# FOX projections of four heads as Strassen chunks in a hybrid decoder block

## The chip, the cores and the metric

The kernel runs on one core of a Trainium2 chip. Its time is the device time of one execution in microseconds (us). The kernel before took 986.61 us, median of 3 runs (986.29 to 989.09).

## The reference

One decoder block on a batch of 512 tokens with 1024 channels, all in float32. The branch A is a gated delta rule (GDN), branch B is an attention with forgetting (FOX); both have 8 heads of 128 channels. One projection makes the inputs of both.

```python
u = rmsnorm(x, norm_mix_g)
proj = u @ w_in
(gq, gk, gv, gz, ga, gb, fq, fk, fv, ff, gate_a, gate_b) = jnp.split(proj, split_idx, axis=-1)
qkv = silu(causal_depthwise_conv(concat([gq, gk, gv]), gdn_conv_w))
o_a = gated_delta_rule_chunked(qh, kh, vh, g, beta)        # qh, kh: l2norm of the heads of qkv
o_a = rmsnorm(o_a, gdn_norm_g) * silu(gz)
y_a = o_a @ w_proj_gdn
o_b = forgetting_attention(rmsnorm(fq), rmsnorm(fk), fv, log_sigmoid(ff + f_bias))
y_b = o_b @ w_proj_fox
h = x + (sigmoid(gate_a) * y_a + sigmoid(gate_b) * y_b) @ w_out
out = h + square(relu(rmsnorm(h) @ w_up)) @ w_down
```

`fq`, `fk` and `fv` of heads 0 to 3 are 12 of the blocks of 128 columns of `w_in`; they are what the change computes in another way.

## The kernel before

**Precision and weight units.** A float32 operand is split into a high part (rounded by a cast on ACT) and a low part (the rest, a subtraction on DVE), and a product is the sum of three: hi by hi, hi by lo, lo by hi. Weights come in units of 128 x 1024. `seq` (L151) lists all units in the order of their use. `unit` fetches the next one, splits up to two units ahead of it (`LA_SPLIT`) and loads up to three ahead (`LA_RAW`). The split halves live in four buffers each (pool `whl`), the raw units in three (`wraw`). L256 is the cast, L257 the subtraction.

**Dense projections.** `dense` (L269) multiplies one unit with all 512 tokens: 24 matmuls of 512 columns (L275, L276 with the high weights, L279 with the low ones), into one of three PSUM banks that take turns. `project` uses it for one of q, k, v of a GDN head and then runs the convolution: ACT L596, three DVE steps L599 that read the bank, silu on ACT. `zgate` uses it for one head's z gate. While u isn't complete, z gates are made from the unscaled x (`xh`, `xl`) and multiplied with the norm on DVE afterwards (L1080); the first `NZX` are made so.

**u.** `normalise` (L411) scales x on POOL, makes the high parts of u on ACT (L289), the low ones on DVE (L290, tiles `ulo`), and stores x scaled to DRAM (`ud`). `factors_u` (L427) loads it back as `ux`, scales it on ACT (L436), adds and subtracts quarters on DVE (L448) and splits the sums (L286, L287). These are the sums of u that Strassen's products need.

**Strassen chunks.** A chunk is a projection to 512 columns for all 512 tokens. As a 2 x 2 problem of blocks it takes seven products P1 to P7 in place of eight. `stream` (L981) runs them: a product is one weight unit and 24 matmuls of 256 columns (L1011) into a kept PSUM bank; after it a quarter of the result is copied out (ACT, L991) or added to what is there (DVE, L993). Four weight blocks of a chunk are stored so that each factor is the last one plus another block: P1 and P2 are plain loads on SP's queue, and P5, P6, P4 (on P1) and P3, P7 (on a plain load) are made by DMAs of POOL's queue that add to the raw unit in SBUF (L219) once it has been split.

**FOX projections before.** Heads 0 to 3 go through `fox_pair` (L950), two heads at a time: three panels of 256 columns, each of two weight units and four blocks of 128 tokens, 24 matmuls of 256 columns per block (L961, L962, L964). Heads 4 to 7 are three chunks of `stream`, followed by four chunks of the gates.

**The order.** The program runs tasks (Python generators) that are advanced by `tick` beside the main line: `head` (transposes, decay products kk and kq), `group_chain` (the inversion of the triangular matrices by 31 column steps of two DVE instructions, L681 and L683, and then the scan), `fox_worker` (attention of FOX heads). The main line is: z gates 0 to 5; GDN group 0 (heads 0 to 3); FOX pair 0; start of `factors_u`; FOX pair 1; z gates 6 and 7; GDN group 1; the stream of seven chunks with the first merges; merges; MLP. Which instruction stands where on each engine is decided when the program is built, by the framework's planner with its own timeline; on the chip each engine then runs its list in that order. `INV_STEP` tells after how much estimated DVE work the inversion of each group pauses until the next `tick`.

Of the kernel before, what the change touches and what calls it, by code (L numbers as in the profile page):

```python
# [15 lines left out]
P = 128  # L16
# [14 lines left out]
NZX = 6  # L31
DC = 2
IN_AT = 6
# [3 lines left out]
NZ1 = 6  # L37
# [3 lines left out]
INV_STEP = (2500, 900)  # L41


def hybrid_block(tc, a, out):
# [99 lines left out]
    def store_late(dst, src):  # L144

        for _ in range(LATE):
# [5 lines left out]
    seq += [("w_gdn", i) for i in range(12)] + [("w_fox", i) for i in range(12)]  # L152
    seq += [("w_z", i) for i in range(NZ1, H)] + [("w_gdn", 12 + i) for i in range(12)]
# [3 lines left out]
    NST = 7  # L157
    STREAM = [("P1", 0), ("P2", 0), ("P5", 0), ("P1", 1), ("P3", 0), ("P6", 0), ("P2", 1), ("P7", 0), ("P5", 1),
              ("P4", 0), ("P3", 1), ("P6", 1)]
    STREAM += [e for c in range(2, NST)  # L160
               for e in (("P1", c), ("P2", c), ("P7", c - 1), ("P5", c), ("P4", c - 1), ("P3", c), ("P6", c))]
    STREAM += [(None, 0), ("P7", NST - 1), (None, 1), ("P4", NST - 1)]
    seq += [(p, ("w_st", c, 0)) if p else ("w_pg", c) for p, c in STREAM]
# [786 lines left out]
    def fox_pair(hp):  # L950
        vts = ([], [])
        for pn in range(3):
            us = [unit("w_fox"), unit("w_fox")]
            pg2 = [page(s="fqk"), page(s="fqk")]
            for t2 in range(2):
                ps = mmps("fx")
                for tb in (2 * t2, 2 * t2 + 1):
                    o = ps[:, (tb % 2) * 256:(tb % 2 + 1) * 256]
                    for k in range(KT):
                        w = us[k // 4][0][:, (k % 4) * 256:(k % 4 + 1) * 256]  # L960
                        mm(o, uhi[k][:, cs(tb)], w, start=(k == 0), stop=False)  # L961
                        mm(o, ulo[k][:, cs(tb)], w, start=False, stop=False)  # L962
                    for k in range(KT):
                        mm(o, uhi[k][:, cs(tb)], us[k // 4][1][:, (k % 4) * 256:(k % 4 + 1) * 256], start=False,  # L964
                           stop=(k == KT - 1))
                    if tb % 2 == 0:
                        tick()
                if pn < 2:
                    act.copy(pg2[t2], ps)
                else:  # L970
                    for j in range(2):
                        (vec.tensor_copy if j else act.copy)(
                            v3(pg2[j][:, 2 * t2 * P:(2 * t2 + 2) * P], 2), v3(ps[:, :], 2)[:, :, cs(j)])
                tick()
            if pn < 2:
                fq.append((2 * hp + pn, pg2, vts[pn]))
            else:
                for v, x in zip(vts, pg2):
                    v += [x[:, cs(c)] for c in range(NCH)]

    def stream(parts, other):  # L981
# [13 lines left out]
        for p, c in STREAM:  # L995
# [143 lines left out]
    v45, v67 = ([], []), ([], [])  # L1139
# [380 lines left out]
```

## Time and profile before

| | |
|---|---|
| median of 3 runs | 986.61 us |
| profiled execution, its own time | 985.26 us |
| its span, first to last instruction | 983.6 us |
| granted TensorE clock | 1.00 |
| PE busy | 971.4 us, 6545 matmuls |
| DVE busy | 714.8 us |
| ACT busy | 602.4 us |
| POOL busy | 243.5 us |

By stage, from the trace: the norm and six z gates end at 48.28 us, GDN group 0 at 126.75, the FOX pairs at about 218, z gates 6 and 7 and group 1 at 328, the stream at about 548, and the rest runs to 983.6. In these six stretches PE was busy for 45.74 of 48.28, 77.84 of 78.47, 91.63 of 92.25 (to 219), 105.13 of 109.00, 219.57 of 220.00 and 431.44 of 435.60 us.

In rows of the profile, PE is TensorE's matmul, DVE VectorE, ACT ScalarE, POOL GpSimd, SP SyncE. A group's row gives line, engine, operation, output and inputs, shape and count, then the busy time and mean ns of one, then the idle time before it and who ended it. Durations of neighbouring matmuls overlap, since they are pipelined, so what one costs is read from the distance of starts. `[1.74 <-DVE conv L599]` is idle time of the engine just before the instruction and what it waited for.

### The profile page before, as it was taken

What the parts mean: (1) busy time and instruction counts of PE and PEld (TensorE: products, weight loads), DVE (VectorE), ACT (ScalarE), POOL (GpSimd) and SP (SyncE); (2) the same over time, 40 slices, a digit from 0 to 9 for tenths busy, and PEclk for the clock granted to TensorE, in tenths of its full rate; (3) what the DMA queues carried; (4) which work ended last, traced back from release to release, by engine and by line L of the source; (5) the groups of instructions that cost most, each with busy time, mean ns of one, the idle gap of its engine ahead of it and who ended that gap; (6) DMA issues with size and microseconds to landing.
All of it is one profiled execution on the core that took longest, in us unless ns stands there. A gap on an engine that the chain in (4) does not pass through costs nothing.

```text
span 983.6 us, 17196 instructions
## 1 busy us (share of the span) xinstructions
PE 971.4 (99%) x6545; PEld 875.7 (89%) x6545; DVE 714.8 (73%) x1205; ACT 602.4 (61%) x1048; POOL 243.5 (25%) x236
## 2 busy tenths in 40 slices
PE   9999999999999999999999999999999999999998
PEld 7878899998877999999999888889989989988986
DVE  6877768557577789854656625889897697698596
ACT  7766454676455687777666522578855765666761
POOL 1555020020623613512230004412021121121110
PEclk9999999999999999999999999999999999999999
DMA  7647653456338776756887835688798888888884
GB/s 265 219 142 216 180 157 108 129 193 204 118 104 240 175 162 160 190 131 156 241 194 204 288 107 164 121 187 166 199 174 202 189 173 208 179 174 203 187 166 119
DMA packets 93442, 174.38 MB, mean 177 GB/s; under 512 B 8016, under 2 KB 49200, under 8 KB 93360
## 3 DMA queue, kind: packets, MB, share of 16 engines
q1 hardware_dynamic: 78928, 120.85, 38.3%
q0 software_dynamic: 14432, 52.44, 30.5%
q8 instruction: 51, 0.84, 0.3%
q14 instruction: 31, 0.25, 0.1%
HBM read 152.25 MB, written 21.02 MB: 176 GB/s over the span
## 4 chain that ended last, share of the span: by engine, by line
PE 91%; DVE 4%; ACT 2%; DMA 2%; issue 1%; SPq 0%; DVEq 0%
PE mlp L1171 35%; PE st L1011 13%; PE mm L279 8%; PE mm L275 7%; PE mm L276 7%; PE fx L964 2%; PE fx L961 2%; PE fx L962 2%; PE fo L944 2%; PE sc L919 1%; PE pT L935 1%; DVE lo L257 1%; DMA ux<-ud 1%; DVE ulo L290 1%; PE v L797 1%; PE o L818 1%
## 5 line engine op out<-in xcount | busy, mean ns | idle before, releaser
L1402 ACT CAST hi<-draw 128x1024 fp32r<-128x1024 f32 x124 | 130.1, 1050 | 118.4 <-PE mlp L1171 102.5
L1409 DVE TENSOR_TENSOR lo<-draw,hi 128x1024 fp32r<-128x1024 f32 x124 | 151.4, 1222 | 44.7 <-ACT hi L1402 41.8
L256 ACT CAST hi<-raw 128x1024 fp32r<-128x1024 f32 (+1 forms) x62 | 62.7, 1020 | 91.3 <-PE mm L276 67.5
L1171 PE MATMUL mlp<-hi,shi 128*128 128x512 f32 x280 | 109.6, 391 | 0.1
L1171 PE MATMUL mlp<-hi,slo 128*128 128x512 f32 x280 | 109.2, 390 | 0.0
L1171 PE MATMUL mlp<-lo,shi 128*128 128x512 f32 x280 | 109.1, 389 | 0.0
L257 DVE TENSOR_TENSOR lo<-raw,hi 128x1024 fp32r<-128x1024 f32 (+1 forms) x62 | 75.8, 1228 | 28.6 <-PE mm L279 12.5
L1171 PE MATMUL mlp<-shi,lo 128*128 128x256 f32 x448 | 90.4, 283 | 0.0
L1171 PE MATMUL mlp<-shi,hi 128*128 128x256 f32 x448 | 90.4, 283 | 0.0
L1171 PE MATMUL mlp<-slo,hi 128*128 128x256 f32 x448 | 90.4, 283 | 0.0
L275 PE MATMUL mm<-uhi,hi 128*128 128x512 f32 x208 | 82.3, 396 | 3.9 <-DVE conv L599 3.9
L276 PE MATMUL mm<-ulo,hi 128*128 128x512 f32 x208 | 81.6, 392 | 0.0
L257 DVE TENSOR_TENSOR lo<-sraw,hi 128x1024 fp32r<-128x1024 f32 x49 | 60.7, 1239 | 21.9 <-ACT hi L256 19.0
L1171 PEld LDWEIGHTS mlp<-shi,hi 128*128 128x128 f32 x448 | 70.7, 192 | 0.9
L256 ACT CAST hi<-sraw 128x1024 fp32r<-128x1024 f32 x49 | 51.4, 1048 | 30.4 <-PE st L1011 17.3
L1171 PEld LDWEIGHTS mlp<-shi,lo 128*128 128x128 f32 x448 | 69.9, 192 | 0.0
L1171 PEld LDWEIGHTS mlp<-slo,hi 128*128 128x128 f32 x448 | 69.9, 192 | 0.0
L1171 PEld LDWEIGHTS mlp<-hi,shi 128*128 128x128 f32 x280 | 52.6, 188 | 11.2 <-issue 0.7
L1171 PEld LDWEIGHTS mlp<-lo,shi 128*128 128x128 f32 x280 | 52.6, 188 | 11.0
L1171 PEld LDWEIGHTS mlp<-hi,slo 128*128 128x128 f32 x280 | 52.6, 188 | 10.4
L599 DVE SCALAR_TENSOR_TENSOR conv<-mm,c_conv,conv 128x509 f32<-128x509 f32 (+2 forms) x72 | 52.3, 743 | 10.4 <-ACT conv L596 9.5
L219 POOL DMA_DIRECT2D draw<-w_d x30 | 26.3, 876 | 129.7 <-DVE lo L1409 127.4
(335 smaller groups left out, 2452.9 us busy)
## 6 DMA issues: line engine op xcount, KB each, us to landing
draw<-w_u POOLq DMA_DIRECT2D x32, 512.0 KB, 5.7
draw<-w_d POOLq DMA_DIRECT2D x32, 512.0 KB, 5.7
sraw<-w_st POOLq DMA_DIRECT2D x28, 512.0 KB, 6.0
draw<-w_d SPq DMA_DIRECT2D x26, 512.0 KB, 4.5
raw<-w_gdn SPq DMA_DIRECT2D x24, 512.0 KB, 3.7
draw<-w_u SPq DMA_DIRECT2D x24, 512.0 KB, 4.3
sraw<-w_st SPq DMA_DIRECT2D x21, 512.0 KB, 5.0
hd<-hd SPq DMA_DIRECT2D x34, 256.0 KB, 5.6
```

The lines of the kernel that those rows point to most:

```text
L219: nc.gpsimd.dma_start(raw, a[w][c, q, s_], accum_op=ALU.add)
L256: act.copy(hi[:, c], raw[:, c])
L257: vec.tensor_tensor(lo[:, c], raw[:, c], hi[:, c].bitcast(F32), op=ALU.subtract)
L275: mm(o, w, rhi(k), start=(k == 0), stop=False)
L276: mm(o, w, rlo(k), start=False, stop=False)
L279: mm(o, lo[:, k * cols:(k + 1) * cols], rhi(k), start=False, stop=(k == KT - 1))
L599: vec.scalar_tensor_tensor(y[:, s:], ps[:, :T - s], cw[:, i:i + 1], y[:, s:], op0=ALU.mult, op1=ALU.add)
L944: mm(po[:, cs(i)], vt[c], st[i][:, cs(c)], start=(c == 0), stop=(c == i))
L1011: mm(o, u, w, start=first and t == 0 and k == 0 and j == 0 and x is hi, stop=x is lo and k == 3, skip_group_check=True)
L1171: return (lambda *args, **kw: tc.keep_in_program_order(f(*args, **kw))) if self.pinned[0] else f
L1402: pact.copy(hi, raws[m][0])
L1409: pvec.tensor_tensor(lo, raws[m][0], hi[:, :].bitcast(F32), op=ALU.subtract)
```

## The change

Three chunks, with the weights of heads 0 to 3, go in front of the list of chunks, and `stream` takes its order of products as an argument. It now runs twice: chunks 0 to 2 between the two GDN groups, where the FOX pairs were, with z gates 6 and 7 in the two places that the second stream gives to merges; and chunks 3 to 9 where the stream was. `fox_pair` and `w_fox` are gone. `factors_u` starts after head 1 of group 0 and has to be finished before the first stream. The z gate of head 5 moves behind group 0, where u is complete. `IN_AT` is 9 in place of 6 because chunks are numbered from the new ones. The inversion of group 0 pauses after as little work as that of group 1.

```diff
-NZX = 6
+NZX = 5
-IN_AT = 6
+IN_AT = 9
-NZ1 = 6
+NZ1 = 5
-INV_STEP = (2500, 900)
+INV_STEP = (900, 900)
...
-    seq += [("w_gdn", i) for i in range(12)] + [("w_fox", i) for i in range(12)]
-    seq += [("w_z", i) for i in range(NZ1, H)] + [("w_gdn", 12 + i) for i in range(12)]
+    seq += [("w_gdn", i) for i in range(12)] + [("w_z", i) for i in range(NZ1, H - 2)]
...
+    STREAMS = chunks(0, 3), chunks(3, 10)
+    seq += [(p, ("w_st", c, 0)) if p else ("w_z", H - 2 + c) for p, c in STREAMS[0]]
+    seq += [("w_gdn", 12 + i) for i in range(12)]
+    seq += [(p, ("w_st", c, 0)) if p else ("w_pg", c) for p, c in STREAMS[1]]
...
-    def gdn_group(g, box):
+    def gdn_group(g, box, also=None):
...
+            if also and i == also[0]:
+                also[1]()
...
-    def fox_pair(hp):
...
-        for p, c in STREAM:
+        for p, c in order:
...
-    ch0 = gdn_group(0, box)
-    fox_pair(0)
-    fu = start(factors_u())
-    fox_pair(1)
+    fus = []
+    ch0 = gdn_group(0, box, (1, lambda: fus.append(start(factors_u()))))
+    fu, = fus
+    zs = list(range(NZ1, H))
+    while len(zs) > 2:
+        zgate(zs.pop(0))
+    finish(fu)
+    v45, v67, v01, v23 = [([], []) for _ in range(4)]
+    parts = [fox_chunk((None, v01), (0, v01[0])), fox_chunk((2, v23[0]), (1, v01[1])), fox_chunk((3, v23[1]), (None, v23)),
+             fox_chunk((None, v45), (4, v45[0])), fox_chunk((6, v67[0]), (5, v45[1])), fox_chunk((7, v67[1]), (None, v67))]
+    stream(STREAMS[0], parts, lambda: zgate(zs.pop(0)))
     start(decays(1, box, ch0))
     hold[0] = True
-    for h in range(NZ1, H):
-        zgate(h)
     ch1 = gdn_group(1, box)
     hold[0] = False
-    finish(fu)
...
-    stream(parts, merge_gdn)
+    stream(STREAMS[1], parts, merge_gdn)
```

What the planner makes of it, at three places. First PE at the start of GDN group 0, behind the z gate of head 4. `xs`, `hi` and `lo` in the inputs are x, `uhi` and `ulo` are u. Before, the z gate of head 5 stands here:

```order
L275 MATMUL mm_594<-xs_197,hi_518 128x512
L276 MATMUL mm_594<-xs_197,hi_518 128x512
L275 MATMUL mm_594<-xs_198,hi_518 128x512
L276 MATMUL mm_594<-xs_198,hi_518 128x512
L275 MATMUL mm_594<-hi_228,hi_518 128x512
L276 MATMUL mm_594<-lo_229,hi_518 128x512
```

Now it is the first projection of head 0, with the second one mixed in:

```order
L279 MATMUL mm_596<-uhi_182,hi_518 128x512
L280 MATMUL mm_596<-ulo_190,hi_518 128x512
L279 MATMUL mm_596<-uhi_183,hi_518 128x512
L279 MATMUL mm_647<-uhi_179,hi_553 128x512
L280 MATMUL mm_647<-ulo_187,hi_553 128x512
L280 MATMUL mm_596<-ulo_191,hi_518 128x512
L279 MATMUL mm_596<-uhi_184,hi_518 128x512
L279 MATMUL mm_647<-uhi_180,hi_553 128x512
L280 MATMUL mm_596<-ulo_192,hi_518 128x512
```

The first user of u moved 24 matmuls forward on PE; `ulo_187` to `ulo_194` are the eight tiles of u's low half.

Second, PE behind group 0. Before, a FOX block:

```order
L279 MATMUL mm_1267<-uhi_186,lo_1136 128x512
L961 MATMUL fx_1323<-hi_1206,uhi_179 128x256
L962 MATMUL fx_1323<-hi_1206,ulo_187 128x256
L961 MATMUL fx_1323<-hi_1206,uhi_180 128x256
L962 MATMUL fx_1323<-hi_1206,ulo_188 128x256
```

Now P1 of chunk 0, behind the z gate of head 5 (`mm_1349`):

```order
L283 MATMUL mm_1349<-uhi_186,lo_1218 128x512
L986 MATMUL st_1423<-hi_1284,uhi_179 128x256
L986 MATMUL st_1423<-hi_1284,uhi_180 128x256
L986 MATMUL st_1423<-hi_1284,uhi_181 128x256
L986 MATMUL st_1423<-hi_1284,uhi_182 128x256
L986 MATMUL st_1423<-hi_1284,ulo_187 128x256
```

A weight unit now serves 24 matmuls in place of 48, and the next product needs the next unit. Third, DVE at the same time in the program. Before, with FOX units (`lo`), convolutions and the decay products of head 3:

```order
L599 SCALAR_TENSOR_TENSOR conv_1244<-mm_1212,c_conv,conv_1244 128x509
L650 SCALAR_TENSOR_TENSOR am_1289<-kq_1284,ssk_1163,em_826 128x128 x4
L257 TENSOR_TENSOR lo_1316<-raw_1313,hi_1315 128x1024
L599 SCALAR_TENSOR_TENSOR conv_1303<-mm_1267,c_conv,conv_1303 128x511
L599 SCALAR_TENSOR_TENSOR conv_1303<-mm_1267,c_conv,conv_1303 128x510
L599 SCALAR_TENSOR_TENSOR conv_1303<-mm_1267,c_conv,conv_1303 128x509
```

Now, with the units of the products (`sraw`) and the sums of u (`ux`):

```order
L261 TENSOR_TENSOR lo_1418<-sraw_1221,hi_1417 128x1024
L603 SCALAR_TENSOR_TENSOR conv_1261<-mm_1223,c_conv,conv_1261 128x509
L291 TENSOR_TENSOR lo_1270<-ux_1244,hi_1269 128x512
L452 TENSOR_TENSOR ux_1245<-ux_1161 128x256
L452 TENSOR_TENSOR ux_1245<-ux_1163 128x256
L291 TENSOR_TENSOR lo_1310<-ux_1245,hi_1309 128x512
L654 SCALAR_TENSOR_TENSOR am_1318<-kq_1313,ssk_1174,em_791 128x128 x4
L261 TENSOR_TENSOR lo_1458<-sraw_1421,hi_1457 128x1024
L452 TENSOR_TENSOR ux_1245<-ux_1244,ux_1161 128x256
L603 SCALAR_TENSOR_TENSOR conv_1332<-mm_1290,c_conv,conv_1332 128x511
```

The convolutions of the last head now stand behind splits and sums that were elsewhere before or not there at all.

More of the change, by code (lines that the diff above doesn't have):

```diff
@@ L151, in hybrid_block, with chunks @@
     seq = [("w_ab", 0)] + [("w_z", i) for i in range(NZ1)]
-    seq += [("w_gdn", i) for i in range(12)] + [("w_fox", i) for i in range(12)]
-    seq += [("w_z", i) for i in range(NZ1, H)] + [("w_gdn", 12 + i) for i in range(12)]
[L157 to L163, printed above, removed]
+    seq += [("w_gdn", i) for i in range(12)] + [("w_z", i) for i in range(NZ1, H - 2)]
+    def chunks(c0, c1):
+        o = [("P1", c0), ("P2", c0), ("P5", c0), ("P1", c0 + 1), ("P3", c0), ("P6", c0), ("P2", c0 + 1), ("P7", c0),
+             ("P5", c0 + 1), ("P4", c0), ("P3", c0 + 1), ("P6", c0 + 1)]
+        o += [e for c in range(c0 + 2, c1)
+              for e in (("P1", c), ("P2", c), ("P7", c - 1), ("P5", c), ("P4", c - 1), ("P3", c), ("P6", c))]
+        return o + [(None, 0), ("P7", c1 - 1), (None, 1), ("P4", c1 - 1)]
+    STREAMS = chunks(0, 3), chunks(3, 10)
+    seq += [(p, ("w_st", c, 0)) if p else ("w_z", H - 2 + c) for p, c in STREAMS[0]]
+    seq += [("w_gdn", 12 + i) for i in range(12)]
+    seq += [(p, ("w_st", c, 0)) if p else ("w_pg", c) for p, c in STREAMS[1]]
     seq += [("w_pg", i) for i in range(2, KT)] + [("w_pf", i) for i in range(KT)]
@@ L948, in fox_worker, with stream @@
             stores.append(start(store_late(obd[h], o)))
-    def fox_pair(hp):
[L951 to L981, printed above, removed]
+    def stream(order, parts, other):
         bank = {}
@@ L1137, in merge_gdn @@
         tick()
-    v45, v67 = ([], []), ([], [])
-    parts = [fox_chunk((None, v45), (4, v45[0])), fox_chunk((6, v67[0]), (5, v45[1])), fox_chunk((7, v67[1]), (None, v67))]
     parts += [gate_chunk(i, to) for to in (sga, mg) for i in range(2)]
-    stream(parts, merge_gdn)
+    stream(STREAMS[1], parts, merge_gdn)
     ot2 = start(outputs_in2())
```

13 lines of the change are left out of this document (4 added, 9 removed).

## The prediction

> **What bounds the kernel now.** I read the head of the page first, then the engines of the chain that ended last, then the waits of PE in front of matmuls (us in total, times, longest).
>
> ```profile
> span 983.6 us, 17196 instructions
> PE 971.4 (99%) x6545; PEld 875.7 (89%) x6545; DVE 714.8 (73%) x1205; ACT 602.4 (61%) x1048; POOL 243.5 (25%) x236
> PE 91%; DVE 4%; ACT 2%; DMA 2%; issue 1%; SPq 0%; DVEq 0%
> PE mm L275 <- DVE conv L599: 3.9, 2, 2.1
> PE cum L511 <- DVE gf L506: 0.6, 1, 0.6
> ```
>
> PE is busy for 971.4 of 983.6 us and carries 91% of the chain. So a change can do two things: take matmuls away, or make or end a wait of PE, and all waits in the span are only 12.2 us. DVE at 714.8 us is second; it matters where a stage makes it work without pause. The profiled execution took 985.26 us (1.66 around the span); the median, 986.61, lies 1.35 above. My sum goes against 985.26, and 1.35 is added at the end.
>
> **Term 1, the matmuls.** The PE timeline (start, us, instruction) at the first FOX block and at the first Strassen product, and the groups of the FOX lines:
>
> ```profile
> 126.75 0.28 PE L961 MATMUL fx<-hi,uhi 128*128 128x256 f32 x1
> 128.67 1.12 PE L964 MATMUL fx<-lo,uhi 128*128 128x256 f32 x8
> 129.63 0.60 PE L119 MATMUL ktm<-ident,conv 128*128 128x128 f32 x4
> ...
> 327.99 0.64 PE L1011 MATMUL st<-hi,uhi 128*128 128x256 f32 x4
> 330.86 0.38 PE L119 MATMUL ktm<-ident,conv 128*128 128x128 f32 x2
> ...
> L961 PE MATMUL fx<-hi,uhi 128*128 128x256 f32 x192 | 48.5, 289 | 0.0
> L962 PE MATMUL fx<-hi,ulo 128*128 128x256 f32 x192 | 47.8, 284 | 0.0
> L964 PE MATMUL fx<-lo,uhi 128*128 128x256 f32 x192 | 28.4, 286 | 0.0
> ```
>
> A FOX block of 24 matmuls runs from 126.75 to 129.63: 2.88 us, 0.120 each. A product, also 24 of the same size, runs from 327.99 to 330.86: 2.87, 0.1196 each. Printed durations (0.28) overlap; starts give the price. Removed: 3 x 192 = 576. Added: 3 chunks x 7 products x 24 = 504. Difference 72 x 0.12 = **-8.6 us**. These matmuls were back to back on PE, so nothing hid them.
>
> **Term 2, the start of group 0.** The z gate of head 5 moves behind group 0. Its 24 matmuls cost the same there (and it loses the DVE multiplication L1080, 0.68). But it was also the work between the norm and the first user of its output. PE there, and DVE making the low halves of u:
>
> ```profile
> 42.73 0.40 PE L275 MATMUL mm<-xs,hi 128*128 128x512 f32 x1
> 48.28 0.39 PE L275 MATMUL mm<-uhi,hi 128*128 128x512 f32 x1
> 53.15 0.43 PE L511 MATMUL cum<-gf,upper 128*128 128x64 f32 x2 [0.63 <-DVE gf L506]
> ...
> 44.19 0.74 DVE L290 SCALAR_TENSOR_TENSOR ulo<-x,c_norm_mix_g,uhi 128x512 fp32r<-128x512 f32 x1
> 46.09 1.41 DVE L290 SCALAR_TENSOR_TENSOR ulo<-x,c_norm_mix_g,uhi 128x512 fp32r<-128x512 f32 x2
> 47.55 0.74 DVE L290 SCALAR_TENSOR_TENSOR ulo<-x,c_norm_mix_g,uhi 128x512 fp32r<-128x512 f32 x1
> 48.61 0.74 DVE L290 SCALAR_TENSOR_TENSOR ulo<-x,c_norm_mix_g,uhi 128x512 fp32r<-128x512 f32 x1
> 49.27 0.68 DVE L1080 TENSOR_TENSOR proj<-mm,rb 128x512 f32<-128x512 f32 x1
> ```
>
> Group 0 began at 48.28; now it can begin at 42.73. The L290 rows from 44.19 make tiles 3, 4 and 5, 6, 7 of the low half (order on DVE and ACT unchanged to here), done at 44.93, 46.83, 47.50, 48.29 and 49.35. PE takes one of its 512-wide matmuls per 0.23 us (24 from 42.73 to 48.28). In the order, tile 3 comes after 7 matmuls: 42.73 + 1.6 = 44.3, so it waits 0.6. Tile 4 comes after 4 more: 44.93 + 0.92 = 45.85, waits 1.0. Tiles 5 to 7 then come within 0.2 of being ready, because a second projection is mixed in. Some 0.1 for each hand-over: **+2.0 us**; ends 0 (all early) and 6.6 (nothing overlapped: 49.35 - 42.73).
> **Term 3.** The 0.63 us that PE waited at 53.15 for gf goes, since PE now arrives two later at the same place of its order: **-0.6** (0 to -0.6).
>
> **Term 4, DVE in the first stream.** The FOX pairs asked little of DVE: 60.86 of 92.25 us (third of the pairs after the span, by PE, PEld, DVE, ACT, POOL).
>
> ```profile
> 126.75:219.00 92.25, 91.63 (x930) 89.55 (x929) 60.86 (x147) 52.97 (x107) 14.27 (x13) 1.00 0.48 149
> 345.00:400.00 55.00, 55.00 (x438) 52.52 (x437) 51.21 (x137) 43.60 (x93) 16.57 (x17) 1.00 0.70 161
> L257 DVE TENSOR_TENSOR lo<-sraw,hi 128x1024 fp32r<-128x1024 f32 x49 | 60.7, 1239 | 21.9 <-ACT hi L256 19.0
> L287 DVE TENSOR_TENSOR lo<-ux,hi 128x512 fp32r<-128x512 f32 x8 | 6.3, 791 | 4.9 <-ACT hi L286 4.9
> L448 DVE TENSOR_TENSOR ux<-ux,ux 128x256 f32<-128x256 f32 x12 | 5.3, 480 | 0.1
> L599 DVE SCALAR_TENSOR_TENSOR conv<-mm,c_conv,conv 128x509 f32<-128x509 f32 x24 | 17.8, 743 | 0.5
> L993 DVE TENSOR_TENSOR fqk<-fqk,st 128x512 f32<-128x512 f32 x9 | 6.1, 672 | 2.5 <-ACT fqk L991 2.5
> L681 DVE TENSOR_TENSOR tmp<-E,X 128x126 f32<-128x126 f32 x6 | 1.7, 286 | 0.1
> 113.35 1.23 DVE L257 TENSOR_TENSOR lo<-raw,hi 128x1024 fp32r<-128x1024 f32 x1 [2.08 <-PE mm L279]
> 114.49 0.16 DVE L617 TENSOR_SCALAR ssk<-ssk 128x4 f32<-128x4 f32 x1
> ```
>
> In place of 12 weight units there are 21, each split by an ACT cast and a DVE subtraction: 9 x 1.24 = 11.2 us more on DVE. The sums of u (16 L448 at about 0.48 and 8 L287 at 0.79: 14) move ahead, into group 0 and the stream's start. Their eight loads from DRAM pass SP's queue in group 0, where three raw buffers stand ahead of use; they are needed some 30 us later. Nine evictions by addition (0.67) take the place of four copies, 5 us more at most. All this comes to 30 us in a stage with 31 us of pause. ACT, with 52.97 of 92.25, gets nine casts; POOL, with 14.27, twelve DMA issues: both have room.
> I counted the DVE order between two rows: from behind the split of the z unit ahead of the stream, to the split of the 19th product. There are 131 instructions: 19 splits (23.5 us), 12 sums (5.8), 7 splits of them (5.5), 12 conv steps (8.9), 7 evictions (4.7), 41 column steps of the inversion at about 0.29 (11.9), and the heads' and attention's own (18.7): 79 us by group means. A row starts about 0.08 before the printed end of the last (48.61 + 0.74 against 49.27 above), so 131 rows take about 69 by starts. PE's work between the uses of the same two splits is 58 us (19 products of 2.87, the rest transposes and attention). DVE's lead is about 14 us: a unit split from 113.35 is first used by its low half at 128.67, and the 2.08 us ahead of that split was a wait for a free buffer. So 69 to 79 stand against 58 + 14 = 72: from 3 us spare to 7 short. The tightest place is the second product, whose bank is freed by group 0's last conv step, 42nd of these rows: by my sum DVE is there between 0.5 ahead and 4 late. A DVE without pause need not stall PE: in 345 to 400 it was busy for 51.21 of 55.00, PE for all 55.00. I take **+1.5**; ends 0 and 12.4 (the last rival).
>
> **Term 5, conv waits of group 1.**
>
> ```profile
> 286.43 0.47 PE L275 MATMUL mm<-uhi,hi 128*128 128x512 f32 x1 [1.74 <-DVE conv L599]
> 308.32 0.47 PE L275 MATMUL mm<-uhi,hi 128*128 128x512 f32 x1 [2.13 <-DVE conv L599]
> ```
>
> Both waits of L275, 1.74 and 2.13, are PE waiting for a bank that a conv step on DVE still reads; DVE had paused before each (for the sums of ACT and for buffers) and then had a head's whole work at once. In the new order the decay matrices of group 1 and its heads' products stand later and closer together, so both bursts remain in some form; by hand I find about 0.8 and 2: **-0.9**, ends -3.9 (both gone) and +4 (doubled).
> **Term 6, the second stream.** The wider spread of group 0's column steps and attention pushed behind put 94.9 us of DVE (group means) beside 92.5 of PE in its first part, before 86.9 beside 87.3. The buffers allow three products of lead, 8.6 us, so it should hide: **+0.5**, ends 0 and 3. The tail (gates, merge, MLP) has the same order at the same distances: 0; without its cover it would wait as long as group 1's chain comes late, and 29 us of products lie between.
> Sum: -8.6 + 2.0 - 0.6 + 1.5 - 0.9 + 0.5 = -6.1, 979.2 for the profiled execution, **980.5 us** against the median.
>
> **One rule against the change.** Two rows at the same time:
>
> ```profile
> 277.48 2.33 DVE L257 TENSOR_TENSOR lo<-raw,hi 128x1024 fp32r<-128x1024 f32 x1 [1.10 <-PE mm L279]
> 277.43 1.30 POOL L588 TENSOR_TENSOR eb<-em,row 128x512 f32<-128x512 f32 x1
> ```
>
> The split took 2.33 instead of 1.24 while POOL multiplied: 1.1 us lost. The Trainium skill, "SBUF — State Buffer", section "Who interferes with whom", says that a DVE instruction with two SBUF inputs and a GpSimd instruction that reads SBUF exclude each other for a whole instruction; this pair of rows agrees. By that rule all the added splits and sums are open to such collisions; rival (c) has the price.
>
> **Rivals.** (a) **No difference**: the first stream stalls 6 us, at the second product and again at the sixth, whose weight comes out of two accumulations one after the other.
>
> ```profile
> L219 POOL DMA_DIRECT2D sraw<-w_st x28 | 24.8, 886 | 92.1 <-DVE lo L257 64.6 <-DVE X L683 12.7 <-DVE fsm L931 9.0
> sraw<-w_st POOLq DMA_DIRECT2D x28, 512.0 KB, 6.0
> ```
>
> Each such step may start only when DVE has split the weight below it, and then takes 0.89 to issue and 6.0 to land; POOL waited 64.6 us for such splits already (L219's idle time). A late DVE is passed on to PE about 7 us later. For it: the -3 to +7 above. Then -6.1 + 4.5 = -1.6, and about 985. Against it: in 345 to 400 the same chain ran beside a full DVE.
> (b) **Better**: the stream hides all and both conv waits vanish: -8.6 + 2.0 - 0.6 - 3.9 = -11.1, 975.5. For it: DVE's pauses of 2.08 before 113.35 are room.
> (c) **Slower**: DVE becomes the bound of the first stream. If the means (79) hold, because POOL blocks the splits as at 277.48, and the lead is only the three products that the buffers give (8.6), PE waits 79 - 58 - 8.6 = 12.4: -8.6 + 1.4 + 12.4 - 0.4 = +4.8, 991.4. It decides from about 8 us of waiting in the stretch. The order has nine POOL tensor operations beside these rows; nine collisions at 1.1 make 10, just the distance between 69 and 79. Against it: the mean of the 49 product splits, 1.239, is next to the single undisturbed 1.23 at 113.35, so few of them met POOL.
> (d) The change not doing what it says: the order has 72 matmuls fewer, so 0.01.
>
> **How the numbers follow.** Forecast 0.56 (977.5 to 983.6: the small terms by their nearer ends), (a) 0.20, (b) 0.14, (c) 0.09, rest 0.01. The range 975 to 988 leaves out (c), the lower part of (b) and the top of (a). Within 0.3% (983.65 to 989.57), about what a measurement of this kernel can tell from no change: (a), 0.20. Faster: forecast and (b), 0.70. Slower: (c) and the rest, 0.10.
>
> **What would show it.** Term 1: 72 fewer matmuls, 504 more rows on the product line, at 0.12 each. Term 2: first projection of group 0 near 42.7 with waits on ulo of 1 to 3 us. Term 4: in the 60 us after the last projection of group 0, waits of products on conv or lo under 3 us in total, with DVE over 85% busy; (a) shows 6, (c) over 10 and many L257 rows above 1.5 us. Term 5: conv waits in group 1 of 1 to 4 us. I am wrong if PE's total idle time grows by more than 6 us, or if it grows in a place that I called hidden.

## The result: slower by 0.8%, and the profile after

The changed kernel takes 992.85 us (median of 6 runs, 992.03 to 996.08), the kernel before 986.3 us (6 runs, 984.68 to 989.09). The ratio is 1.0076, with a 95% interval of 1.0061 to 1.0091. The forecast was 980.5 us; the difference to it is 12.3 us. The profiled execution of the changed kernel has a span of 990.6 us, 7.0 more than before. Two lines of its page (busy time, share of the span and instructions of each engine):

```profile
span 990.6 us, 17122 instructions
PE 968.1 (98%) x6473; PEld 869.3 (88%) x6473; DVE 725.7 (73%) x1218; ACT 614.3 (62%) x1059; POOL 254.2 (26%) x248
```

And the three longest of PE's waits in it (engine, tile and line that wait, what ended the wait; us in total, times, longest):

```profile
PE st L986 <- DVE fqk L968: 3.6, 1, 3.6
PE st L986 <- ACT fqk L966: 2.9, 3, 1.6
PE mm L279 <- DVE conv L603: 2.5, 1, 2.5
```

There are 72 matmuls fewer, as forecast, but PE's busy time fell by 3.3 us, not by 8.6, and the waits are others: most are not in the first stream but inside group 1 and at the start of the second stream. The stages show it. These are the windows (stretch, its length, then PE, PEld, DVE, ACT and POOL busy, the granted clock, the DMA share and GB/s) of the kernel before and then of the changed one:

```profile
125.00:200.00 75.00, 74.38 (x780) 72.17 (x780) 51.37 (x130) 41.00 (x84) 13.37 (x12) 1.00 0.42 124
280.00:360.00 80.00, 76.13 (x491) 68.45 (x490) 63.99 (x131) 50.19 (x122) 31.59 (x27) 1.00 0.69 177
```

```profile
125.00:200.00 75.00, 73.23 (x632) 70.53 (x630) 67.14 (x149) 49.43 (x93) 22.35 (x22) 1.00 0.80 179
280.00:360.00 80.00, 69.60 (x426) 61.57 (x425) 53.61 (x104) 47.59 (x112) 41.71 (x35) 0.94 0.63 152
```

In 125 to 200, where the first stream runs, DVE went from 51.37 to 67.14 of 75 us and PE lost 1.15 us. In 280 to 360, from the middle of group 1 into the second stream, PE lost 6.5 us more than before, and the clock was 0.94. For a sum over the span I took each step from one matmul's start to the next one's, minus the median step, over all runs of this document, of matmuls of the same shape into the same tile. What is above the median is called lost time here, by wait or by slow matmuls (us):

| stretch | 0 to 125 | 125 to 200 | 200 to 280 | 280 to 360 | from 360 | sum |
|---|---|---|---|---|---|---|
| before | 5.2 | 0.3 | 0.3 | 4.6 | 3.0 | 13.4 |
| changed | 6.5 | 1.9 | 1.3 | 15.7 | 3.4 | 28.9 |

So 15.5 us of new loss stand against 8.6 us of matmuls saved, which makes the 7 us by which the span grew, and 11.1 of them lie in 280 to 360. In the PE timeline of the changed kernel there (start, busy time of the group in us, line, operation, tiles, shape, count, and in brackets the wait ahead of it and what ended it):

```profile
298.19 0.77 PE L279 MATMUL mm<-uhi,hi 128*128 128x512 f32 x1 [2.47 <-DVE conv L603]
299.61 0.63 PE L280 MATMUL mm<-ulo,hi 128*128 128x512 f32 x1
...
324.54 0.71 PE L986 MATMUL st<-hi,uhi 128*128 128x256 f32 x4 [1.27 <-DVE conv L603]
332.75 0.33 PE L905 MATMUL fkT<-ident,fqk 128*128 128x128 f32 x1 [1.25 <-DVE AT L645]
337.31 1.23 PE L986 MATMUL st<-hi,uhi 128*128 128x256 f32 x4 [3.58 <-DVE fqk L968]
342.42 0.64 PE L986 MATMUL st<-hi,hi 128*128 128x256 f32 x4
```

The second stream starts at 324.54; before it was 327.99, so up to there the change is still 3.45 us ahead. Then PE waits 1.25 and 3.58 us, and behind the second wait the matmuls run at little more than half speed: 24 of them from 337.31 to 342.42, 0.213 us each where 0.120 is usual, 2.2 us more. The granted clock is 0.50 from 335.35 to 342.17 and 1.00 from 342.20 to 346. The same at 298.19: seven matmuls take about 0.43 each in place of 0.23.

Why DVE was late at 337 is read from the order of the heads. The products kk of heads 4, 5 and 6 of group 1 stand on PE at these times before and after:

```profile
281.37 1.05 PE L639 MATMUL kk<-conv 128*128 128x128 f32 x8
298.77 1.05 PE L639 MATMUL kk<-conv 128*128 128x128 f32 x8
320.70 1.05 PE L639 MATMUL kk<-conv 128*128 128x128 f32 x8
```

```profile
308.12 1.06 PE L643 MATMUL kk<-conv 128*128 128x128 f32 x8
311.74 1.06 PE L643 MATMUL kk<-conv 128*128 128x128 f32 x8
317.67 1.05 PE L643 MATMUL kk<-conv 128*128 128x128 f32 x8
```

Three heads that were 17 and 22 us apart now stand 4 and 6 us apart. Each needs rows from DRAM through three buffers, two products on POOL and eight on DVE. Two pieces of the chain of waits of the changed kernel through this stretch:

```profile
315.06 9.86 DMA row<-rowd
325.07 1.31 POOL conv L656
```

Its POOL timeline there, and its DVE timeline:

```profile
325.06 1.30 POOL L656 TENSOR_TENSOR conv<-conv,row 128x512 f32<-128x512 f32 x1 [2.48 <-DMA row<-rowd]
326.31 3.03 POOL L895 TENSOR_TENSOR fqk<-fqk,fss 128x512 f32<-128x512 f32 x2
330.08 1.45 POOL L592 TENSOR_TENSOR eb<-em,row 128x512 f32<-128x512 f32 x1
```

```profile
331.57 1.12 DVE L645 SCALAR_TENSOR_TENSOR AT<-kk,ssk,eb 128x128 f32<-128x128 f32 x4 [3.13 <-POOL eb L592]
336.58 0.67 DVE L968 TENSOR_TENSOR fqk<-fqk,st 128x512 f32<-128x512 f32 x1
```

A row load took 9.86 us, and POOL stood 2.48 us for it with its other work queued behind: the product that reads the row, two products `fqk` in 3.03 us and the issue of a weight step. So POOL reached the next head's `eb` only at 330.08; DVE waited 3.13 us for that at 331.57, with decay products, a split, convolution steps and the eviction `fqk` queued behind, and PE waited for that eviction until 337.31. That these loads and POOL's queue are what the closeness of the heads costs is read from this trace; no run changes the loads or their buffers alone.

### The profile page after: what moved, and what is told of

It reads as the page before. It is cut to its first block, busy times and chain, and to the rows that moved or that the text cites. A ratio compares the mean times of both kernels' runs of the same rounds, so it can differ in the third digit from the quotient of the medians.

```text
span 990.6 us, 17122 instructions
## 1 busy us (share of the span) xinstructions
PE 968.1 (98%) x6473; PEld 869.3 (88%) x6473; DVE 725.7 (73%) x1218; ACT 614.3 (62%) x1059; POOL 254.2 (26%) x248
## 4 chain that ended last, share of the span: by engine, by line
PE 91%; DMA 3%; DVE 2%; ACT 1%; issue 1%; POOL 1%; SPq 0%; POOLq 0%; ACTq 0%; DVEq 0%
PE mlp L1148 36%; PE st L986 19%; PE mm L279 8%; PE mm L280 8%; PE mm L283 8%; PE fo L950 2%; DMA row<-rowd 2%; PE sc L925 2%; PE pT L941 1%; DMA sraw<-w_st 1%; PE o L822 1%; PE v L801 1%; PE S L810 1%; DMA raw<-w_z 1%; DVE ulo L294 1%
## 5 line engine op out<-in xcount | busy, mean ns | idle before, releaser
L261 DVE TENSOR_TENSOR lo<-sraw,hi 128x1024 fp32r<-128x1024 f32 x70 | 87.4, 1249 | 24.1 <-ACT hi L260 17.4
L260 ACT CAST hi<-sraw 128x1024 fp32r<-128x1024 f32 x70 | 73.2, 1047 | 48.0 <-PE st L986 26.0
L279 PE MATMUL mm<-uhi,hi 128*128 128x512 f32 x216 | 86.4, 402 | 2.6 <-DVE conv L603 2.5
L280 PE MATMUL mm<-ulo,hi 128*128 128x512 f32 x216 | 85.9, 398 | 1.1 <-DVE ulo L294 1.1
L260 ACT CAST hi<-raw 128x1024 fp32r<-128x1024 f32 (+1 forms) x50 | 50.5, 1013 | 56.3 <-PE mm L280 45.3
L261 DVE TENSOR_TENSOR lo<-raw,hi 128x1024 fp32r<-128x1024 f32 (+1 forms) x50 | 59.1, 1182 | 29.2 <-ACT hi L260 13.9
L223 POOL DMA_DIRECT2D sraw<-w_st x40 | 35.5, 888 | 141.5 <-DVE lo L261 53.4
L1148 PEld LDWEIGHTS mlp<-lo,shi 128*128 128x128 f32 x280 | 52.6, 188 | 11.1
```

Source lines behind the costliest of these rows:

```text
L223: nc.gpsimd.dma_start(raw, a[w][c, q, s_], accum_op=ALU.add)
L260: act.copy(hi[:, c], raw[:, c])
L261: vec.tensor_tensor(lo[:, c], raw[:, c], hi[:, c].bitcast(F32), op=ALU.subtract)
L279: mm(o, w, rhi(k), start=(k == 0), stop=False)
L280: mm(o, w, rlo(k), start=False, stop=False)
L1148: return (lambda *args, **kw: tc.keep_in_program_order(f(*args, **kw))) if self.pinned[0] else f
```

## The experiments

All ratios are against runs of the kernel before on the same chip. Two theories were left at the start. **A**: the change of `INV_STEP` makes group 0's inversion and scan late; group 1's decay matrices wait for the end of that chain. **B**: the added splits and sums are too much for DVE.

### The pauses of the inversion

```diff
 # the changed kernel, pauses of 2500 (and, in another kernel, of 1500)
-INV_STEP = (900, 900)
+INV_STEP = (2500, 900)
```

> The changed kernel with one number put back: the inversion of group 0 pauses after 2500 instead of 900 units of DVE work. Theory A (the many pauses make group 0's inversion and scan end late, so the decay matrices of group 1 come late, the decay products of heads 4 to 6 stand close together, and their DVE work holds up the second stream): in the order the first decay matmul of group 1 moves forward by 25 us of PE work and the kk products of heads 4 to 6 are 14 and 20 us apart instead of 4 and 6; the 11 us that the changed kernel loses between 320 and 360 us go, and the time is 978 to 983 us. Rival B (DVE is over its limit because of the added splits and sums): the column steps now press into the first stream in longer pieces, PE waits more there, and the time stays at 990 us or above.

Measured: 992.59 us, ratio 1.0068 (1.0045 to 1.0090). The heads are spread and the loss in 280 to 360 is 2.4 us, as A said; but the time is that of the changed kernel, as B said. The loss has moved into 125 to 200, 16.7 us, and most of it is one wait, for the inversion's transposed result, with some 2 us of slow matmuls behind it. In its waits of PE:

```profile
PE Qp L711 <- DVE Xd L693: 11.8, 1, 11.8
```

In the timelines of PE and of DVE:

```profile
171.93 0.36 PE L986 MATMUL st<-lo,uhi 128*128 128x256 f32 x1
184.07 1.92 PE L711 MATMUL Qp<-Xd,AT 32*32 32x32 f32 x64 [11.78 <-DVE Xd L693]
```

```profile
182.96 1.06 DVE L693 STREAM_TRANSPOSE Xd<-X 128x512 f32<-128x512 f32 x1
```

And in the windows of the 44 us ahead (columns as above):

```profile
140.00:160.00 20.00, 18.37 (x154) 18.16 (x154) 18.25 (x40) 11.86 (x18) 4.54 (x6) 1.00 0.83 209
160.00:184.00 24.00, 12.29 (x104) 12.09 (x102) 22.07 (x59) 9.12 (x14) 6.07 (x6) 0.84 0.71 174
```

The plan puts the 64 small matmuls Qp behind a product that ends at 172. DVE finishes the column steps at 183, and it was busy 40.3 of the 44 us before. PE runs its list in order, so it stands for 11.8 us.

```diff
 # the kernel before, pauses of 900
-INV_STEP = (2500, 900)
+INV_STEP = (900, 900)
```

> The kernel before with only the pauses of the inversion of group 0 changed, 2500 to 900; the FOX pairs stay. Theory A: group 0's chain ends late without any Strassen product in the place of the pairs, the decay matrices of group 1 come 24 us of PE work later, heads 4 to 6 stand close together, and the kernel becomes slower than before by 6 to 14 us: 992 to 1000 us. Rival B (added splits and sums on DVE): none are added here, 985 to 989 us.

Measured: 1003.03 us, ratio 1.0171 (1.0146 to 1.0196). With the FOX pairs in place and no added split, the one number costs 16 us: 13.4 us are lost in 280 to 360 (4.6 before) and 9.5 behind it (3.0 before). The chain runs through row loads there too (5.92 and 5.73 us). The small matmuls Qp, which read the inversion's result, stand at these times on PE in the kernel before, in the kernel before with pauses of 900, and in the changed kernel:

```profile
179.33 1.20 PE L707 MATMUL Qp<-Xd,AT 32*32 32x32 f32 x64
199.55 1.20 PE L707 MATMUL Qp<-Xd,AT 32*32 32x32 f32 x64
198.95 1.20 PE L711 MATMUL Qp<-Xd,AT 32*32 32x32 f32 x64
```

So the pauses alone make group 0's chain 20 us late, and the late chain is enough for such a loss.

> The changed kernel with pauses of the inversion of group 0 after 1500 units of DVE work, between 900 and 2500. Theory A: the kk products of heads 4 to 6 are 7 and 18 us apart in the order (900: 4 and 6; 2500: 14 and 20), so most of the loss goes: 980 to 986 us. Rival B: 989 us or above.

Measured: 1014.38 us, ratio 1.0283 (1.0259 to 1.0307), the slowest of all. It has both kinds of wait: 5.6 us for the inversion's result, and 4.5 us inside group 1 and 9.0 at its end for convolutions. A had given 980 to 986 us; B's 989 or above holds. How far the heads stand apart in the plan doesn't alone foretell the loss.

```diff
 # the changed kernel, z gates 6 and 7 behind the first stream
-    STREAMS = chunks(0, 3), chunks(3, 10)
+    STREAMS = [e for e in chunks(0, 3) if e[0]], chunks(3, 10)
...
     start(decays(1, box, ch0))
     hold[0] = True
+    while zs:
+        zgate(zs.pop(0))
```

> The changed kernel with z gates 6 and 7 behind the first stream instead of inside it, as cover of 11 us between the start of the task of group 1's decay matrices and group 1; pauses stay at 900. Theory A: that task waits for the end of group 0's chain, which is not moved by it; kk of heads 4 to 6 stand 5 and 4 us apart; 990 to 996 us. Rival C (what was lost is the 11 us of cover that the z gates gave ahead of group 1): 980 to 984 us.

Measured: 996.23 us, ratio 1.0104 (1.0078 to 1.0130). The loss in 280 to 360 stays, at 16.7 us: the lost cover of the z gates is not the cause.

### Less work for DVE

```diff
 # 20 of the 31 column steps of group 0 left out (in three kernels)
-        for j in range(B - 1):
+        for j in range(B - 1 if inverted[0] else 11):
```

> The changed kernel with 20 of the 31 column steps of group 0's inversion left out (pauses at 900): 40 DVE instructions, about 12 us, less in the first stream, and all that hangs on the inversion earlier. Theory A3 (the first stream asks more of DVE than it has time for, so group 0's inversion, and with it group 0's scan and group 1's decay matrices, end late; PE pays for that lateness wherever the plan puts it): the loss of 14 us goes for the most part; 977 to 984 us. Rival D (each new order of the planner has its own accidental waits, DVE's load has no part in it): 988 to 996 us, with a wait of 5 us or more.

> The same left out in the kernel with pauses of 2500, whose one large wait was 11.8 us for the inversion's result. Theory A3: 12 us of DVE less, but the planner also puts the waiting matmuls 7 us earlier; the wait falls to 3 to 7 us and the time to 980 to 988 us. Rival D: no relation; 990 us or above is as likely as below.

> The same left out in the kernel before, as a control. Theory A3: DVE has room in the FOX pairs, so taking 12 us from it brings little, at most the two conv waits: 981 to 987 us. If the kernel before also gains 8 us or more, the inversion is a bound of both and not of the changed kernel alone.

Measured: 980.93 us (ratio 0.9961, 0.9948 to 0.9974), 986.04 us (1.0009, 0.9994 to 1.0025) and, in the kernel before, 987.24 us (1.0022, 1.0007 to 1.0038). The two longest waits of the first and the one of the second that counts, each from the view of PE's waits:

```profile
PE mm L279 <- DVE conv L603: 1.9, 3, 1.3
PE st L986 <- ACT fqk L966: 1.9, 2, 1.6
```

```profile
PE Qp L711 <- DVE Xd L693: 3.6, 1, 3.6
```

Without those steps the changed kernel takes 11 to 12 us less than with them, and the loss in 280 to 360 is 1.2 us. That its time is the forecast's is in part luck: it loses 6.3 us in 125 to 200, where the forecast had 1.5 more than before. The wait for the inversion falls from 11.8 to 3.6 us with pauses of 2500. The kernel before gains nothing from the same edit. So the loss hangs on when the inversion ends. With pauses of 900 this doesn't tell DVE's work from the pauses, since fewer steps also mean fewer pauses; the next two kernels do.

```diff
 # no low split for 9 of the 21 products of the first stream
+            if nme in ("P4", "P6", "P7") and i[0] == "w_st" and i[1] < 3:
+                act.copy(hi, raw)
+                units.append((hi, hi))
+                continue
             lo = whl.tile([P, D], F32R, tag="lo", name=nm("lo"))
```

> The kernel with pauses of 2500 without the low split of P4, P6 and P7 of the first stream (9 of 21 products, as many as the change added units; their matmuls take the high part twice, so PE has the same work and the low part is left out of the result). Six of these splits, 6.8 us of DVE, stand ahead of the inversion's end. Theory A3 (DVE's added work in the first stream is what PE waits for at the inversion's result): the wait of 11.8 us falls to 4 to 6 us and the time to 983 to 987 us. If it stays at 10 us or more, the added splits aren't the cause.

> The same left out in the changed kernel with its pauses of 900. Here the plan itself puts the inversion's result late (PE work 181 instead of 184), because its pieces wait for the next product each, and group 1's decay matrices stay where they were. Theory A3, completed: with 900 the lateness is made by the pauses, whatever DVE has to do, so the loss behind 280 us stays: 989 to 994 us. If DVE's load alone made it, 980 to 986 us.

Measured: 985.64 us (ratio 1.0000, 0.9989 to 1.0010) and 990.46 us (1.0053, 1.0034 to 1.0071). With pauses of 2500 the wait falls by 4 us, to 7.8, and the time by 7. With pauses of 900 the loss in 280 to 360 stays at 15.0 us, and Qp still stands at 193.24. Both causes are real: DVE's added work holds up the inversion where the plan lets it run, and where the plan gives it pauses, the pauses alone make it late, and taking work from DVE helps little.

### An earlier release of the decay matrices

```diff
 # decays(1) waits for n steps of group 0's scan, not for the whole chain
-        while after is not None and after in tasks:
+        while after is not None and not (scanned[0] >= n or after not in tasks):
```

> The changed kernel, pauses at 900 as it has them, but the task of group 1's decay matrices waits for the first step of group 0's scan instead of the end of group 0's whole chain. Theory A2 (DVE is full in the first stream, so group 0's chain can't end earlier than it does in the changed kernel; the loss comes only from what is tied to that end): group 0's inversion stands where it stood (PE work 184), the first decay matmul of group 1 moves forward by 42 us of PE work and kk of heads 4 to 6 are 18 and 16 us apart instead of 4 and 6. No waits on Xd in the first stream, waits of group 1 and of the start of the second stream under 4 us together: 977 to 983 us. Rival B2 (the added DVE work is the loss itself and only shows at another place when things are moved, as between the changed kernel and the one with pauses of 2500): 989 us or above, with a new wait of 8 us or more somewhere.

> The changed kernel with the decay matrices of group 1 released after the second step of group 0's scan, between the first (991.5 us, one wait of 8.4) and the third (988.1 us, waits of 4.0 and 1.6 to 1.3). If the loss is what is late of group 0 landing among group 1's convolutions, the time lies with its neighbours: 986 to 992 us. If the release alone mattered, 980 to 985 us.

> The changed kernel with the decay matrices of group 1 released after the third step of group 0's scan (the first step moved the loss to one wait of 8.4 us for a conv step in group 1 and gained 1 us). If the loss is the scan's own late work landing on DVE and ACT among group 1's convolutions, it stays: 988 to 994 us. If it was only the place of the decay matrices, which now stand 15 us of PE work ahead of the changed kernel's: 980 to 986 us.

> The kernel before with the same edit alone: the task of group 1's decay matrices waits for the first step of group 0's scan. Theory A2: in the kernel before the heads are already spread (kk 15, 19 and 23 us apart, now 19, 19 and 23), so there is little to win: the two conv waits of 3.9 us may shrink; 982 to 987 us. If it gained as much as in the changed kernel (over 6 us), the release would be a gain of its own and not the cause of the changed kernel's loss.

Measured: after the first step 991.54 us (ratio 1.0046, 1.0029 to 1.0063), the second 993.66 us (1.0085, 1.0064 to 1.0107), the third 988.06 us (1.0022, 1.0011 to 1.0033); in the kernel before, first step, 987.96 us (1.0020, 1.0006 to 1.0034). The third step takes 4.8 us off the changed kernel and is the best of the versions that leave nothing out, but slower than before. The first doesn't reach the 977 to 983 us that theory A2 gave for it, nor do the others, and in the kernel before the release gains nothing. The loss in 280 to 360 is 10.6, 16.0 and 9.0 us, in each case mostly one or two waits for a convolution in group 1. For the first step, a row of PE's waits and two of DVE's timeline:

```profile
PE mm L279 <- DVE conv L604: 8.4, 1, 8.4
```

```profile
300.35 0.17 DVE L622 TENSOR_SCALAR ssk<-ssk 128x4 f32<-128x4 f32 x1 [0.86 <-ACT junk L612]
308.80 4.68 DVE L604 SCALAR_TENSOR_TENSOR conv<-mm,c_conv,conv 128x511 f32<-128x511 f32 x7
```

DVE does a head's work, two convolution steps and a split from 300.35 on and then seven convolution steps in one piece: nine steps, those of the three projections in the three banks, while PE waits for a bank. So the place of the decay matrices is a part of the loss, and group 0's scan and its output work, which now fall among group 1's convolutions, can be another. Why the second step is worse than its neighbours I can't say.

```diff
 # release after the third step, and six z gates ahead of group 0
-NZX = 5
+NZX = 6
-NZ1 = 5
+NZ1 = 6
```

> Release after the third step, and six z gates ahead of group 0 as in the kernel before (the seventh and eighth in the first stream). The wait for u at the start of group 0 (1.1 us) goes, group 0 and all behind it starts a z gate later. By the start alone: 986 to 988 us. If the tightness in group 1 grows with the lateness of group 0, 988 to 994 us.

Measured: 996.82 us, ratio 1.0133 (1.0104 to 1.0162). That is 9 us more than with the z gate behind group 0. Without it the first stream waits 3.1 us for a convolution at 137.92, with 1.6 us of slow matmuls behind it; the rest lies in 200 to 280, with a wait of 4.3 us for POOL at 279.81, and how that hangs on the z gate isn't shown. Term 2 had priced the move of that z gate at a loss of 2.0 us and nothing else.

### DVE work moved elsewhere

```diff
 # pauses of 2500; sums of u, and low parts of P4 and P7, on POOL
-                    vec.tensor_tensor(x[:, o], in0, in1, op=op)
+                    pool.tensor_tensor(x[:, o], in0, in1, op=op)
...
+                sub = pool if ... else vec
+                sub.tensor_tensor(lo[:, c], raw[:, c], hi[:, c].bitcast(F32), op=ALU.subtract)
```

> The changed kernel with pauses of 2500, with the 16 sums of u and the low parts of the units of P4 and P7 of the first stream made on POOL instead of DVE (same results). About 9 us of DVE work leave the stretch before the inversion's end. Theory A3: the wait of 11.8 us falls to 3 to 6 us: 982 to 987 us, faster than or equal to the kernel before. If POOL and DVE stand in each other's way at their inputs, DVE instructions of that stretch get longer and the wait stays over 8 us: 989 us or above.

Measured: 991.82 us, ratio 1.0079 (1.0062 to 1.0097). The wait for the inversion is 11.4 us, hardly less than 11.8. Two of POOL's splits in its timeline, and DVE's instructions beside them in its own:

```profile
150.76 2.66 POOL L262 TENSOR_TENSOR lo<-sraw,hi 128x1024 fp32r<-128x1024 f32 x1
168.87 2.52 POOL L262 TENSOR_TENSOR lo<-sraw,hi 128x1024 fp32r<-128x1024 f32 x1 [1.89 <-ACT hi L260]
```

```profile
150.03 0.24 DVE L686 TENSOR_TENSOR tmp<-E,X 128x81 f32<-128x81 f32 x1
150.31 3.23 DVE L688 TENSOR_TENSOR X<-X,tmp 128x81 f32<-128x81 f32 x1
169.18 2.36 DVE L686 TENSOR_TENSOR tmp<-E,X 128x128 f32<-128x128 f32 x1
```

An instruction of a column step that takes 0.24 to 0.30 takes 2.4 to 3.2 us beside a split on POOL. Three of POOL's four splits ahead of the inversion's end meet one; they cost DVE 8 us more and took 3.4 us of splits from it. What the moved sums gave beside that isn't worked out.

```diff
 # sums of u after head 0 of group 0 (with pauses of 2500; and with the release after the first step)
-    ch0 = gdn_group(0, box, (1, lambda: fus.append(start(factors_u()))))
+    ch0 = gdn_group(0, box, (0, lambda: fus.append(start(factors_u()))))
```

> The changed kernel with pauses of 2500 (which waited 11.8 us for the inversion's result in the first stream) and the sums of u after head 0 instead of head 1. If that wait is DVE's total work between the last convolutions and the inversion's end, moving some 8 us of sums and splits out of it takes 5 to 9 us off the wait: 984 to 988 us. If the wait has another cause (the planner's place for the inversion's last steps), it stays at 10 us or more and the time at 991 to 994 us.

> As the first kernel of this call, and the sums of u start after head 0 of group 0 instead of after head 1. In DVE's order 16 sums and 8 splits then end 12 rows after the first product's split instead of 46 rows after it. Theory A2: the first stream hid this DVE work already, waits there were 1.6 us; the time is within 2 us of the first kernel. Rival B2: it wins 4 us or more.

Measured: 1002.50 us (ratio 1.0161, 1.0142 to 1.0179) and 1000.98 us (1.0157, 1.0128 to 1.0185). Both lose 11 to 12 us more up to 125 us, where convolutions now wait behind sums: 2.5 and 7.8 us, 2.5 and 7.2 us. In the second, DVE is busy for 19.6 of the 22 us from 92 on. The first keeps a wait of 10.6 us for the inversion, so my expectation for it fell. In this order there is no room ahead of the first stream for 8 us of sums.

```diff
 # pauses of 2500; z gates 6 and 7 ahead of the first stream
-    while len(zs) > 2:
+    while zs:
```

> The kernel with pauses of 2500, with z gates 6 and 7 ahead of the first stream instead of at its end (all results as the reference's). They are 11 us of PE work with two splits, in place of four products with four splits and two evictions, ahead of the inversion's end; the plan puts the inversion's result 4 us of PE work later. Theory A3: DVE gets 7 to 9 us more time ahead of that place, the wait falls to 2 to 5 us: 982 to 987 us. Otherwise 990 us or above.

Measured: 1010.91 us, ratio 1.0249 (1.0223 to 1.0275), where I had expected a gain. The wait for the inversion is 12.9 us; DVE itself waited 4.1 and 2.0 us for casts of the products' weights in this stretch, and group 1 has four waits of its own. Which of the moved loads or casts did it was not tried.

## Why the prediction was wrong

- **Term 1 (-8.6) was right.** There are 72 matmuls fewer, at 0.12 each, and with the new losses of 15.5 us they account for the span.
- **Terms 2 and 3 (+2.0 and -0.6) were right in sum**: 1.3 us more are lost up to 125 us. PE began group 0 at 42.99 and waited 0.38 and 0.71 us for the low part of u, at the fourth and fifth tiles as worked out; the wait for gf is gone. What Term 2 left out is that the moved z gate gives cover ahead of the first stream: the kernel without it takes 9 us more (996.82 against 988.06, both with the release after the third step), of which a wait of 3.1 us is seen there.
- **Term 4 (+1.5) was right in the place and wrong in what it leaves out.** In 125 to 200, 1.6 us more are lost; PE has one long wait, 1.63 us for an eviction, with DVE at 90%. I asked whether DVE's list holds up PE *inside* the stretch. I didn't ask what becomes late behind it. The inversion's result is read on PE only at the end of the stretch, and all of group 0's chain hangs on it. Its end is set mostly by the pauses in the changed kernel (Qp at 198.95, still at 193.24 with nine splits fewer), and by DVE's work with pauses of 2500 (Qp at 184.07 behind a wait of 11.8 us, at 178.81 behind one of 7.8 with nine splits fewer).
- **Terms 5 and 6 are the step that failed (-0.9 and +0.5).** Together they were -0.4 (the waits of 0.8 and 2 that Term 5 names make -1.1, not -0.9); the stretch from 280 to 360 lost 11.1 us more than before. I had the decay matrices later and the heads closer in the order, and priced that as two conv waits of 0.8 and 2. The conv waits came, 2.47 and 1.27 us. What was missing is what three heads one after the other ask of the row loads and POOL's queue, and the wait of 3.58 us that they end in, in the second stream, which I had called hidden by three products of lead. The cause of the lateness, `INV_STEP`, was in the sum only as "the wider spread of group 0's column steps", inside the +0.5; alone it costs the kernel before 16 us.
- **Rival (c), with 0.09, gave 991.4 us, and that this is near is luck.** Its signs didn't come: PE lost under 2 us in the first stream, and none of the 18 product splits in 125 to 200 took over 1.23 us, so POOL didn't slow them. Its outcome, PE standing 12.4 us for a DVE without time, is close to what the kernel with pauses of 2500 shows, 11.8 us in one wait, but there too the splits up to the wait take 1.19 to 1.23: it is the amount of DVE's work, not collisions with POOL. Against such a stall Term 4 held that a full DVE in 345 to 400 didn't hold up PE; no inversion's result was waited for in that stretch.
- **A cost that no term had**: the clock after a wait, some 1.5 us at 298.19 and 2.2 us at 337.31.

The two edits, chunks and pauses, give four kernels (medians in us):

| | pauses of 2500 | pauses of 900 |
|---|---|---|
| FOX pairs | 986.3 | 1003.03 |
| Strassen chunks | 992.59 | 992.85 |

So the loss can't be shared out between DVE's added work and the pauses as two numbers. Either one alone costs time, 6 and 16 us, and both together cost no more than the chunks alone, since both make the same chain late. At pauses of 900 the chunks win some 10 us, about the size of Term 1; the change goes from the first of the four numbers to the last. What stays open is how much of each number belongs to one particular order: every edit makes a new plan, and pauses of 1500 (1014.38) and the release after the second step (993.66) are worse than their neighbours for reasons that weren't found.

## What to carry to other kernels

When work is added to an engine that is second in busy time, don't only ask whether the bound engine waits for it in that stretch; ask which of its tasks has no reader there, because that one can be delayed unseen, and follow what hangs on its end. In a kernel whose order is planned ahead, a pause or a release point is a part of the critical path even where it issues no instruction: price it by the chain it delays, by moving it alone in the kernel before. A wait of the bound engine costs more than its length where the clock falls behind it.

## What the hardware showed that I had not expected

**The clock behind a short wait.** In these runs a single wait of PE of 1.76 us or less, alone in its surroundings, was not followed by slow matmuls. From 1.81 us on it mostly was, for 3 to 6 us and at a cost of 1.4 to 2.9 us, whether the wait was 1.8 or 12.9 us long. Between 1.81 and 2.54 both occur. PE's timeline of the last kernel above (z gates ahead) at 312, of the kernel before at 308, and of the kernel before with pauses of 900 at 337:

```profile
312.23 0.47 PE L279 MATMUL mm<-uhi,hi 128*128 128x512 f32 x1 [1.81 <-DVE conv L603]
314.25 0.63 PE L280 MATMUL mm<-ulo,hi 128*128 128x512 f32 x1
```

```profile
308.32 0.47 PE L275 MATMUL mm<-uhi,hi 128*128 128x512 f32 x1 [2.13 <-DVE conv L599]
308.63 0.40 PE L276 MATMUL mm<-ulo,hi 128*128 128x512 f32 x1
```

```profile
337.24 0.71 PE L1011 MATMUL st<-hi,uhi 128*128 128x256 f32 x4 [2.15 <-DVE conv L599]
338.27 1.04 PE L1011 MATMUL st<-lo,uhi 128*128 128x256 f32 x4
...
341.66 0.66 PE L1011 MATMUL st<-hi,uhi 128*128 128x256 f32 x4
```

After 1.81 us the 512-wide matmuls take 0.43 each from 313.8 on; after 2.13 us they go on at 0.23; after 2.15 us groups of four 256-wide ones take 0.85 in place of 0.48. Shorter waits close together were enough too: in the changed kernel with the short inversion waits of 0.68 and 1.04 us left PE busy for 3.08 of the 4.80 us from 174.00 on, and the granted clock was 0.50 in the 3.41 us behind that. The Trainium skill, "TensorE: Matmul & The Clock Gate", section "What's actually happening", tells of an activity window of about 3.4 us that runs freely and halves the clock after an idle one. That the same length of wait does and doesn't slow the matmuls agrees with a window whose phase is free; that a wait of 1.8 us can be enough is less than a whole window, and there the measurement decides.

**POOL and DVE.** The Trainium skill, "SBUF — State Buffer", section "Who interferes with whom", says that a DVE instruction with two SBUF inputs and a GpSimd one that reads SBUF exclude each other for the whole instruction. The rows of the kernel with splits on POOL agree, and show the price: DVE's small step is held until POOL's 2.5 to 2.7 us are over, so moving a split of 1.14 us from DVE to POOL cost DVE more than it freed where the two met.
